# The order of the sums into the first three output tiles of W2, in the 8-tile segments of an MLP

## The chip, the cores and the metric

The kernel runs on one NeuronCore of a Trainium2 chip. The metric is the time of one execution on the device, in microseconds (us), as the median of several runs. A second view is one execution taken by the hardware profiler; all rows below are from that one.

## What is computed

One inference step of a four-layer backbone over 384 tokens (256 latent, 128 context) of width 1024. Layer 0 and 3 mix tokens with a bidirectional state-space layer (S5), layer 1 with neighbourhood attention, layer 2 with grouped-query attention. After each mixer stands the same MLP, and the change lies in it:

```python
def sqrelu_mlp(h, w1, w2):
    a = jax.nn.relu(h @ w1)
    return (a * a) @ w2
...
xp = xp + p_g2 * sqrelu_mlp(hp, mlp_w1[i], mlp_w2[i])
xs = xs + s_g2 * sqrelu_mlp(hs, mlp_w1[i], mlp_w2[i])
```

`w1` is 1024 x 4096, `w2` is 4096 x 1024, all in float32. `h` is the RMS-normed residual stream with scale and shift, `g2` a gate; both come from the conditioning vector (adaLN).

## The kernel before

Features lie on the 128 partitions, the 384 tokens along the free dimension, so the 1024 features of the residual stream `x` are 8 tiles of 128 x 384 and the 4096 hidden features 32 tiles. Each float32 operand is held as two exact parts, a rounded one (`hi`) and the rest (`lo`), and each product is three matmuls (`mm3`, L225: hi x hi, hi x lo, lo x hi, at L227, L228, L229).

Weights come in chunks of 128 x 1024 (`chunk`, L215): SyncE loads one into a `raw` buffer, ScalarE (ACT) casts it to `whi` (L221), VectorE (DVE) subtracts to get `wlo` (L93, the helper of all tensor-tensor operations). There are five raw buffers, which the adaLN weights (`ada`, L163) share, four of `whi` and four of `wlo`.

`mlp` (L385) goes over the hidden features in segments. In layers 0 and 3 there are two segments of 16 hidden tiles. In layers 1 and 2 there are four segments of 8, since tables of the second S5 layer are made beside them (`s5_spill`, L879, on DVE, GpSimd, ACT and PE) and take the space. A segment has two halves:

- W1: for each of its hidden tiles, one chunk of W1 times `h` (24 matmuls into one PSUM bank), then `normed` (L328): DVE multiplies by 1/rms (`nt`) and copies the shift (`nb`), ACT takes the ReLU. DVE squares it (`asq`), and `split` (L231) makes `ahi` (ACT, L235) and `alo` (DVE). These are the squared tiles, a[0] to a[7] in a segment of 8.
- W2: for each of the 8 output tiles f, one chunk of W2 per 8 squared tiles: 24 matmuls, a[0] to a[7] in order, into one bank. Then `residual` (L360; the instructions `x<-mm,mod,x` of L111) adds gate times the bank to `x`. In the last segment of a layer `final` (L280) follows for each tile: ACT and DVE make the next layer's scaled input and the sum of squares (`sq`, `acc`). Where the next layer is S5 (after layer 2), ACT makes `hs` (L294), and after tiles 3 and 7 PE sorts four of them into chunks (`pick`, L357).

From layer 0's mixer on, three PSUM banks serve these sums in turn (`mm`, L239). A bank is free again when DVE has read it: by `nb` in W1, by `residual` in W2. The order of instructions on each engine is set when the program is built, by a scheduler that follows the order of the code closely; every engine runs its own list in order, and an instruction that waits holds up the rest of its list.

Of the kernel before, what the change touches and what calls it, by code (L numbers as in the profile page):

```python
# [18 lines left out]
PSUM = bass.MemoryType.PSUM  # L19
DRAM = bass.MemoryType.DRAM  # L20

P = 128
D = 1024
KT = D // P
# [8 lines left out]
# S5: chunks of Q steps, NC chunk columns (latent 0-15, context 0-15, latent 16-31)  # L33
# [5 lines left out]
# groups per scan; output tiles of the GLU whose first half of the rows comes early  # L39
# [4 lines left out]
# batches of E and of C of the second S5 layer that are made beside the MLP of a layer  # L44
SPILL = {0: (0, 4), 1: (4, 2), 2: (4, 2)}
# steps of adaLN per step of S5, per projection of the neighbourhood and of the grouped-query attention
FS, FN, FG = 4, 2, 1
# steps of attention per projection
SN, SQ = 4, (3, 5, 3)


class Builder:
# [21 lines left out]
    def psum(self, mm, aux, tab=0, sc=0):  # L74
        """PSUM in banks: sums of projections, all else, tables and scores."""
        if self.ps:
            self.ps.close()
        self.ps = ExitStack()
        self.ps_mm = self.pool(self.ps, f"ps_mm{tab}", mm, space=PSUM)
        self.ps_aux = self.pool(self.ps, f"ps_aux{tab}", aux, space=PSUM)  # L80
        if tab:
            self.ps_tab = self.pool(self.ps, "ps_tab", tab, space=PSUM)
        if sc:
            self.ps_sc = self.pool(self.ps, "ps_sc", sc, space=PSUM)
# [29 lines left out]
    def setup(self):  # L114
# [29 lines left out]
        # the q gains carry the scales of the scores  # L144
# [4 lines left out]
    def streams(self, ap):  # L149
        """The two streams of [P, NTOK]: context columns, latent columns."""  # L150
        return (ap[:, 256:], ap[:, 0:256])

# [21 lines left out]
    def flush(self):  # L174
        """The end of the last group of ada()."""
# [55 lines left out]
    def split(self, pool, src, tag, bufs=None):  # L231
        """src as exact hi + lo."""
        hi = pool.tile([P, NTOK], F32R, name=tag + "hi", tag=tag + "hi", **({"bufs": bufs} if bufs else {}))
        lo = pool.tile([P, NTOK], F32R, name=tag + "lo", tag=tag + "lo", **({"bufs": bufs} if bufs else {}))
        self.nc.scalar.copy(hi[:], src)  # L235
        self.sub(lo[:], src, hi[:].bitcast(F32))
        return hi, lo
# [7 lines left out]
    def proj(self, src, x):  # L245
        """One output tile = chunk^T x over the 8 k-tiles of x."""
        hi, lo = self.chunk(src)
        n = x[0][0].shape[1]
        ps = self.mm_tile()[:, :n]
        for k in range(KT):  # L250
            self.mm3(ps, hi[:, k * P:(k + 1) * P], lo[:, k * P:(k + 1) * P], x[k][0][:], x[k][1][:],
                     k == 0, k == KT - 1)
        return ps

# [17 lines left out]
    def scratch(self, start, n):  # L272
        """n values of the space of the norm's parts, where they aren't in use."""
        return self.sc[:, start:start + n]

    def next_norm(self, l, n):
        """The norm that the residual stream goes to next, built up as its tiles become final."""
        self.nx = {"l": l, "n": n, "acc": None, "parts": None, "h": [], "s5": n == 0 and l % 3 == 0}

    def final(self, k):  # L280
        """x[k] is final: x gain as exact parts, the shifts in two more columns, or as chunks for S5; and the sum of
        squares."""
# [37 lines left out]
    def rstd(self):  # L320
        """1 / rms of every token, on all partitions."""
# [6 lines left out]
    def normed(self, pool, ps, r, func, dst):  # L328
        """dst = func(r * ps + shift) from a projection of the parts that final() makes."""
# [9 lines left out]
    def rsqrt(self, m, r):  # L339
        """(m + EPS)^-1/2: a first value from the tables, one Newton step."""  # L340
# [12 lines left out]
    def pick(self, out, gg, src):  # L353
        """out[(step, channel)] = src(step)[channel of group gg], steps in reverse."""
# [5 lines left out]
    def residual(self, ps, gate, f):  # L360
        """x[f] += gate * ps."""
# [3 lines left out]
    def out_proj(self, src, half, x, l, steps, fill):  # L365
        """x += gate * (W^T o) over half of the heads."""
# [18 lines left out]
    def mlp(self, l):  # L385
        nc = self.nc
        with ExitStack() as ctx:
# [17 lines left out]
            for half in range(npart):  # L405
                a = []
                for f in range(seg):
# [6 lines left out]
                    step()  # L414
                for f in range(KT):
                    ps = self.mm_tile()[:, :NTOK]
                    for q in range(seg // KT):
                        hi, lo = self.chunk(self.i["w2"][l, half * seg // KT + q, f])
                        for k in range(KT):
                            kk = q * KT + k  # L420
                            self.mm3(ps, hi[:, k * P:(k + 1) * P], lo[:, k * P:(k + 1) * P], a[kk][0][:], a[kk][1][:],
                                     kk == 0, kk == seg - 1)
                    self.residual(ps, gate, f)
# [7 lines left out]
    def head_rstd(self, pool, raws, kind):  # L431
        """1 / rms over the head dim of up to four raw [P, NTOK] tiles."""
# [9 lines left out]
    def head_norm(self, raw, r, j, gain, kind, t):  # L442
        """t = raw r gain, r that of the j-th tile."""
# [7 lines left out]
    def pipeline(self, items):  # L451
        """Pairs of functions, of which the first runs one ahead: steps that other work is interleaved with."""
# [7 lines left out]
    def steps(self, n):  # L460
        """n steps of the attention that runs beside the projections, and the fill of adaLN."""
# [11 lines left out]
    def value_flip(self, raws, v, first):  # L473
        """v[tok, t, feature] from features by tokens."""
# [3 lines left out]
    def softmax_tail(self, p, total):  # L478
        """p *= 1 / total."""
# [3 lines left out]
    def flip(self, p, n, dst):  # L483
        """dst[key, n, q] = transposes of p [q, n * P]."""
# [117 lines left out]
    def gqa(self, l):  # L602
        nc, i = self.nc, self.i
        with ExitStack() as ctx:
# [13 lines left out]
            def project(first, n, st):  # L618
                """The tiles of k (2) and q (8): projected, then normed, turned and used in steps."""
# [90 lines left out]
    def exp(self, pool, out, x):  # L710
        """exp(x) by 2^n e^r, x within float32's range of exponents."""
# [40 lines left out]
    def s5_tables(self, tp, wide, slot, pe, pc, a8):  # L752
        """Discretised parameters: powers of the step in the order of each direction, for E with B's factor; the matrix of
        Q steps. wide: space for 34 G values."""
# [21 lines left out]
        # f = (A - 1) / lambda  # L776
# [14 lines left out]
        # the order of the steps: the first 64 partitions run forward  # L791
# [16 lines left out]
    def make_e(self, pool, slot, b, pe, work, kf, kp, dd, et):  # L808
        """E[(step, channel), g, r, (direction, state)] = A^j B of GB groups, steps in reverse; and into DRAM the
        products Re(C A^j B) within a chunk, one row of 16 values per (distance, channel)."""  # L810
# [24 lines left out]
        # two groups per product, of which the diagonal blocks count  # L835
# [28 lines left out]
    def make_c(self, cr, b, pc, ca, t):  # L864
        """ca = (Re, -Im) of C A^j."""
# [13 lines left out]
    def s5_spill(self, slot, first, ebs, cbs):  # L879
        """The tables of a later S5 layer, kept in DRAM: steps that other work is interleaved with. The parameters come  # L880
        first, then E and C of some groups."""
# [55 lines left out]
    def s5(self, l, slot):  # L937
# [5 lines left out]
        # places in the scratch space: what final() makes, then the reversed chunks of the second half and y; sel;  # L943
        # the reversed chunks of the first half, then the states that y is made from; kp and d, or sums of states
# [114 lines left out]
    def s5_u(self, pool, u, make=None):  # L1059
        """u[(step, channel), g, chunk], steps in reverse: from x's chunks in layer 0, from those of x gain else."""  # L1060
# [45 lines left out]
    def s5_states(self, ssb, b, et, u, ur, s):  # L1106
        """S[c] = sum over the steps of a chunk of A^j B u for GB groups (columns 48-63 of a group belong to the next)."""
# [28 lines left out]
    def s5_scan(self, pool, s, a8):  # L1136
        """h[c] = A^Q h[c - 1] + S[c] in place: the first value of each stream, then its chunks (latent from 0, context
        from 33); the backward half holds them in reverse."""
# [13 lines left out]
    def s5_out(self, pool, b, ca, tz, u, s, hy, gsb, k):  # L1152
        """The outputs of GB groups: from the state before each chunk and from the chunk itself."""
# [41 lines left out]
    def glu_sums(self, slot, f, halves, k):  # L1195
        """Both output tiles of f over halves of the rows."""
# [12 lines left out]
    def glu_first(self, slot, f, k, part):  # L1209
        """The first half of the rows' share in f's output tiles, and the bias."""  # L1210
# [46 lines left out]
def chunks(w):  # L1257
    """[K * 128, N * 128] weights as [N, 128, K * 128]: one output tile per chunk."""
# [4 lines left out]
def half_chunks(w):  # L1263
    """[1024, N * 256] weights as [N, 2, 128, 4 * 256]: two output tiles over half of the rows per chunk."""
# [4 lines left out]
def lay_out(inp):  # L1269
# [13 lines left out]
    # neighbourhood attention  # L1283
# [18 lines left out]
    # grouped-query attention  # L1302
# [27 lines left out]
    # S5: partitions are (direction, state) or, for the chunks, (step, channel)  # L1330
# [47 lines left out]
```

## Time and profile before

| | us |
|---|---|
| median of 3 runs | 2106.98 |
| lowest and highest run | 2102.32, 2116.06 |
| span of the profiled execution, first to last instruction | 2104.6 |

For the profiled execution the page gives the span; what lies around it is not shown, and the span is 2.4 us under the median. PE is its matmul unit, PEld the loading of weights into it. A row of a timeline has the start, the duration, engine, line, operation, tiles out<-in, and in brackets the idle time before it and what ended it. A PE matmul of 384 columns has a duration of some 0.34 us, but the next one starts after about half of that, so time is counted from start to start. W2 of the eight 8-tile segments begins at 895.3, 974.8, 1054.3 and 1127.2 us (layer 1) and at 1362.6, 1441.4, 1520.9 and 1593.6 us (layer 2).

### The profile page before, as it was taken

Reading aid. Unit: us, or ns where it says so; the run is one execution under the profiler, and the core shown is the slowest. Engines: PE = TensorE matmul, PEld = TensorE weight load, DVE = VectorE, ACT = ScalarE, POOL = GpSimd, SP = SyncE. Lnnn points to the kernel's source line nnn. Section 1 sums busy time; section 2 is a strip of 40 time slices with the busy share of each in tenths; the row PEclk is TensorE's granted clock in tenths of the full one; section 3 lists DMA queues with packets and bytes.
Section 4 is the critical chain, followed back from the end, with each engine's and each line's share of the span. In section 5 each row is a group of like instructions: output and inputs, shape, how many; then the busy total and the mean of one; then the engine's idle time right before and its main releaser. Section 6 shows DMA issues by size and latency. Waiting matters only on the chain. (4 is left out here: it accounts for less than half of the span.)

```text
span 2104.6 us, 35187 instructions
## 1 busy us (share of the span) xinstructions
PE 1980.7 (94%) x13490; PEld 1747.3 (83%) x13490; DVE 1368.2 (65%) x3070; ACT 1029.4 (49%) x2112; POOL 216.4 (10%) x180
## 2 busy tenths in 40 slices
PE   5886899999999999999999999999999878999999
PEld 2554799999987777998999877998997657999999
DVE  7899669856445556856658566856665396674562
ACT  4664656335355555634435555534434477553441
POOL 4443210400000000001111000002111000000000
PEclk8997999999999999999999999999999999999999
DMA  7756654443365555634334532533444575333331
GB/s 286 234 199 238 233 182 152 152 170 120 128 233 192 177 179 193 230 121 154 125 132 163 172 114 98 179 131 128 142 149 156 165 281 221 121 126 125 124 131 67
DMA packets 130823, 348.45 MB, mean 166 GB/s; under 512 B 12800, under 2 KB 48544, under 8 KB 128608
## 3 DMA queue, kind: packets, MB, share of 16 engines
q1 hardware_dynamic: 124160, 338.55, 46.8%
q0 software_dynamic: 1712, 4.05, 0.6%
q10 hardware_dynamic: 4784, 3.61, 0.5%
q8 instruction: 107, 1.75, 0.3%
q14 instruction: 60, 0.49, 0.1%
HBM read 323.22 MB, written 22.94 MB: 164 GB/s over the span
## 5 line engine op out<-in xcount | busy, mean ns | idle before, releaser
L221 ACT CAST whi<-raw 128x1024 fp32r<-128x1024 f32 x340 | 356.4, 1049 | 486.4 <-PE mm L228 422.6
L93 DVE TENSOR_TENSOR wlo<-raw,whi 128x1024 fp32r<-128x1024 f32 x340 | 445.2, 1310 | 197.2 <-ACT whi L221 196.3
L227 PE MATMUL mm<-h,whi 128*128 128x386 f32 x1312 | 453.4, 346 | 0.0
L229 PE MATMUL mm<-h,wlo 128*128 128x386 f32 x1312 | 448.2, 342 | 0.0
L228 PE MATMUL mm<-h,whi 128*128 128x386 f32 x1312 | 446.9, 341 | 0.0
L227 PE MATMUL mm<-ahi,whi 128*128 128x384 f32 x1024 | 350.2, 342 | 10.3 <-ACT ahi L235 10.3
L229 PE MATMUL mm<-ahi,wlo 128*128 128x384 f32 x1024 | 349.3, 341 | 2.8 <-DVE wlo L93 2.8
L228 PE MATMUL mm<-alo,whi 128*128 128x384 f32 x1024 | 349.8, 342 | 1.7 <-DVE alo L93 1.6
L227 PEld LDWEIGHTS mm<-h,whi 128*128 128x128 f32 x1312 | 246.7, 188 | 21.7 <-issue 16.7
L228 PEld LDWEIGHTS mm<-h,whi 128*128 128x128 f32 x1312 | 248.3, 189 | 5.0 <-issue 3.7
L229 PEld LDWEIGHTS mm<-h,wlo 128*128 128x128 f32 x1312 | 247.4, 189 | 5.3 <-issue 4.0
L111 DVE SCALAR_TENSOR_TENSOR x<-mm,mod,x 128x128 f32<-128x128 f32 (+1 forms) x256 | 95.4, 412 | 204.8 <-PE mm L229 204.3
L227 PEld LDWEIGHTS mm<-ahi,whi 128*128 128x128 f32 x1024 | 195.3, 191 | 13.3 <-ACT ahi L235 12.6
L229 PEld LDWEIGHTS mm<-ahi,wlo 128*128 128x128 f32 x1024 | 195.3, 191 | 5.0 <-DVE wlo L93 3.4
L228 PEld LDWEIGHTS mm<-alo,whi 128*128 128x128 f32 x1024 | 195.2, 191 | 5.1 <-DVE alo L93 5.1
L163 PE MATMUL ada<-raw,silu 128*2 128x256 f32 x1536 | 127.1, 407 | 21.1 <-DMA raw<-in_ada_w 16.5
L93 DVE TENSOR_TENSOR nt<-mm,rstd 128x384 f32<-128x384 f32 x164 | 90.6, 553 | 68.1 <-PE mm L229 67.5
L337 ACT ACTIVATE relu<-nt,nb 128x128 f32<-128x128 f32 (+1 forms) x256 | 102.1, 447 | 46.3 <-DVE nb L335 45.9
L235 ACT CAST ahi<-asq 128x384 fp32r<-128x384 f32 x128 | 65.4, 513 | 119.2 <-DVE asq L93 118.8
L93 DVE TENSOR_TENSOR alo<-asq,ahi 128x384 fp32r<-128x384 f32 x128 | 73.0, 572 | 50.3 <-ACT ahi L235 50.2
L163 PEld LDWEIGHTS ada<-raw,silu 128*2 128x2 f32 x1536 | 31.4, 85 | 77.4 <-issue 32.2
L227 PE MATMUL mm<-k,whi 128*128 128x384 f32 x256 | 89.1, 352 | 6.0 <-DVE k L93 2.1
(376 smaller groups left out, 3019.1 us busy)
## 6 DMA issues: line engine op xcount, KB each, us to landing
raw<-in_w SPq DMA_DIRECT2D x256, 512.0 KB, 3.5
raw<-in_ada_w SPq DMA_DIRECT2D x192, 512.0 KB, 4.7
raw<-in_glu SPq DMA_DIRECT2D x32, 512.0 KB, 5.5
tz<-kdr SPq DMA_DIRECT2D x16, 512.0 KB, 5.8
dca<-ca SPq DMA_DIRECT2D x8, 1024.0 KB, 4.3
raw<-in_na_wqk SPq DMA_DIRECT2D x16, 512.0 KB, 4.1
det<-et SPq DMA_DIRECT2D x32, 256.0 KB, 2.6
et<-det SPq DMA_DIRECT2D x32, 256.0 KB, 5.7
```

The costliest lines, as they stand in the source:

```text
L93: self.nc.vector.tensor_tensor(out, a, b, op=op)
L111: self.nc.vector.scalar_tensor_tensor(out, a, s, b, op0=op0, op1=op1)
L163: nc.tensor.matmul(ps[32 * j:32 * j + 2], self.silu[:, k, :], raw[:, 256 * j:256 * j + 256], start=(k == 0), stop=(k == KT - 1))
L221: nc.scalar.copy(hi[:], raw[:])
L227: mm(out, whi, xhi, start=first, stop=False)
L228: mm(out, whi, xlo, start=False, stop=False)
L229: mm(out, wlo, xhi, start=False, stop=last)
L235: self.nc.scalar.copy(hi[:], src)
L337: nc.scalar.activation(o, z, func, bias=b[:, s:s + 1])
```

## The change

In a segment of 8 squared tiles (layers 1 and 2, eight segments in all), the first three output tiles of W2 are opened together: each is summed over a[0] to a[5], one tile after the other, and only then over a[6] and a[7], again one after the other. Tiles 3 to 7, and the segments of 16 in layers 0 and 3, keep their order. The three open tiles hold three banks and three pairs of `whi` and `wlo` until their last two squared tiles are in. The number of matmuls, chunks and other instructions is the same.

```diff
+OPEN, LATE = 3, 2
...
+                opened = OPEN if seg == KT else 0
+                sums = {}
+                for f in range(opened):
+                    sums[f] = self.down(half, f, seg, a, l, range(0, seg - LATE))
                 for f in range(KT):
-                    ps = self.mm_tile()[:, :NTOK]
-                    for q in range(seg // KT):
-                        hi, lo = self.chunk(self.i["w2"][l, half * seg // KT + q, f])
-                        for k in range(KT):
-                            kk = q * KT + k
-                            self.mm3(ps, hi[:, k * P:(k + 1) * P], lo[:, k * P:(k + 1) * P], a[kk][0][:], a[kk][1][:],
-                                     kk == 0, kk == seg - 1)
-                    self.residual(ps, gate, f)
+                    ps = self.down(half, f, seg, a, l, range(seg - LATE, seg), *sums[f]) if f in sums else \
+                        self.down(half, f, seg, a, l, range(seg))
+                    self.residual(ps[0], gate, f)
                     step()
                     if half == npart - 1:
                         self.final(f)
...
+    def down(self, half, f, seg, a, l, tiles, ps=None, w=None):
+        ps = self.mm_tile()[:, :NTOK] if ps is None else ps
+        w = {} if w is None else w
+        for kk in tiles:
+            q, k = divmod(kk, KT)
+            if q not in w:
+                w[q] = self.chunk(self.i["w2"][l, half * seg // KT + q, f])
+            hi, lo = w[q]
+            self.mm3(ps, hi[:, k * P:(k + 1) * P], lo[:, k * P:(k + 1) * P], a[kk][0][:], a[kk][1][:], kk == 0, kk == seg - 1)
+        return ps, w
```

In the order of the changed program the line numbers are two higher for the same code (L229 to L231 are the three matmuls, L95 and L113 stand for L93 and L111). On PE, in the first 8-tile segment of layer 1, the first output tile before the change goes through all eight squared tiles; ahi_9348 is a[5], ahi_9391 a[6], the names after the arrow are operands, the one before it is the bank's tile:

```order
L227 MATMUL mm_9438<-ahi_9348,whi_9441 128x384
L228 MATMUL mm_9438<-alo_9349,whi_9441 128x384
L229 MATMUL mm_9438<-ahi_9348,wlo_9442 128x384
L227 MATMUL mm_9438<-ahi_9391,whi_9441 128x384
L228 MATMUL mm_9438<-alo_9392,whi_9441 128x384
L229 MATMUL mm_9438<-ahi_9391,wlo_9442 128x384
L227 MATMUL mm_9438<-ahi_9434,whi_9441 128x384
```

After the change, at the end of the second open tile's first part (mm_9463), a[0] (ahi_9133) of the third open tile (mm_9488) follows a[5]:

```order
L229 MATMUL mm_9463<-ahi_9348,whi_9466 128x384
L230 MATMUL mm_9463<-alo_9349,whi_9466 128x384
L231 MATMUL mm_9463<-ahi_9348,wlo_9467 128x384
L229 MATMUL mm_9488<-ahi_9133,whi_9491 128x384
L230 MATMUL mm_9488<-alo_9134,whi_9491 128x384
L231 MATMUL mm_9488<-ahi_9133,wlo_9492 128x384
```

The first use of a[6] has moved from place 19 of the 192 matmuls of W2 to place 55, that of a[7] from 22 to 58.

On DVE, in the same W2, the additions to `x` and the making of `wlo` take turns before the change:

```order
L93 TENSOR_TENSOR alo<-asq,ahi 128x384
L111 SCALAR_TENSOR_TENSOR x<-mm,mod_5_6554,x 128x128
L111 SCALAR_TENSOR_TENSOR x<-mm,mod_5_6554,x 128x256
L93 TENSOR_TENSOR wlo<-raw,whi 128x1024
L111 SCALAR_TENSOR_TENSOR x<-mm,mod_5_6554,x 128x128
L111 SCALAR_TENSOR_TENSOR x<-mm,mod_5_6554,x 128x256
L93 TENSOR_TENSOR wlo<-raw,whi 128x1024
```

After it, tile 0's addition still comes first, then the fifth chunk's `wlo`, then two additions and two `wlo`:

```order
L95 TENSOR_TENSOR alo<-asq,ahi 128x384
L113 SCALAR_TENSOR_TENSOR x<-mm,mod_5_6554,x 128x128
L113 SCALAR_TENSOR_TENSOR x<-mm,mod_5_6554,x 128x256
L95 TENSOR_TENSOR wlo<-raw,whi 128x1024
L113 SCALAR_TENSOR_TENSOR x<-mm,mod_5_6554,x 128x128
L113 SCALAR_TENSOR_TENSOR x<-mm,mod_5_6554,x 128x256
L113 SCALAR_TENSOR_TENSOR x<-mm,mod_5_6554,x 128x128
L113 SCALAR_TENSOR_TENSOR x<-mm,mod_5_6554,x 128x256
L95 TENSOR_TENSOR wlo<-raw,whi 128x1024 x2
```

One `wlo` has moved behind the addition of tile 2.

On DVE in the last segment of layer 2, where `final` follows (`acc` is the sum of squares), before the change:

```order
L111 SCALAR_TENSOR_TENSOR x<-mm,mod_5_8869,x 128x128
L111 SCALAR_TENSOR_TENSOR x<-mm,mod_5_8869,x 128x256
L93 TENSOR_TENSOR wlo<-raw,whi 128x1024
L263 TENSOR_TENSOR acc<-sq 128x384
L111 SCALAR_TENSOR_TENSOR x<-mm,mod_5_8869,x 128x128
L111 SCALAR_TENSOR_TENSOR x<-mm,mod_5_8869,x 128x256
L93 TENSOR_TENSOR wlo<-raw,whi 128x1024
L263 TENSOR_TENSOR acc<-acc,sq 128x384
L111 SCALAR_TENSOR_TENSOR x<-mm,mod_5_8869,x 128x128
```

(the first addition shown is tile 1's), and after it (from tile 2's):

```order
L113 SCALAR_TENSOR_TENSOR x<-mm,mod_5_8869,x 128x128
L113 SCALAR_TENSOR_TENSOR x<-mm,mod_5_8869,x 128x256
L95 TENSOR_TENSOR wlo<-raw,whi 128x1024
L265 TENSOR_TENSOR acc<-sq 128x384
L95 TENSOR_TENSOR wlo<-raw,whi 128x1024
L265 TENSOR_TENSOR acc<-acc,sq 128x384
L113 SCALAR_TENSOR_TENSOR x<-mm,mod_5_8869,x 128x128
L113 SCALAR_TENSOR_TENSOR x<-mm,mod_5_8869,x 128x256
```

Two `wlo` and two `acc` now stand between the additions of tiles 2 and 3. The orders of GpSimd and of SyncE's loads are as before.

## Rows read from the trace of the kernel before

**Rows 1.** Page, part 2: granted PE clock in 40 slices, in tenths of full.

```profile
PEclk8997999999999999999999999999999999999999
```

**Rows 2.** Waits of PE from 893 to 1640 us: total us, times, longest us.

```profile
PE mm L227 <- ACT ahi L235: 10.3, 6, 2.2
```

**Rows 3.** Windows, 16 us from each W2 start: us, PE busy (matmuls), clock, DMA share, GB/s.

```profile
895.30:911.30 16.00, 11.97 (x58) 0.89 0.39 132
974.80:990.80 16.00, 16.00 (x92) 1.00 0.34 130
1054.30:1070.30 16.00, 16.00 (x91) 1.00 0.36 129
1127.20:1143.20 16.00, 13.63 (x65) 0.89 0.38 130
1362.60:1378.60 16.00, 12.95 (x61) 0.89 0.37 132
1441.40:1457.40 16.00, 16.00 (x92) 1.00 0.38 130
1520.90:1536.90 16.00, 16.00 (x92) 1.00 0.37 129
1593.60:1609.60 16.00, 13.78 (x59) 0.79 0.46 145
```

**Rows 4.** Timeline of PE, W2 of layer 1's first segment, around a[6] and a[7].

```profile
899.94 0.44 PE L227 MATMUL mm<-ahi,whi 128*128 128x384 f32 x1 [1.34 <-ACT ahi L235]
901.00 0.45 PE L228 MATMUL mm<-alo,whi 128*128 128x384 f32 x1 [0.62 <-DVE alo L93]
...
903.67 1.01 PE L227 MATMUL mm<-ahi,whi 128*128 128x384 f32 x2 [2.06 <-ACT ahi L235]
...
905.76 0.52 PE L227 MATMUL mm<-ahi,whi 128*128 128x384 f32 x1
906.08 0.52 PE L228 MATMUL mm<-alo,whi 128*128 128x384 f32 x1
```

**Rows 5.** Timeline of PE, W2 of layer 1's second segment: end of tile 0.

```profile
978.46 0.34 PE L227 MATMUL mm<-ahi,whi 128*128 128x384 f32 x1
978.79 0.45 PE L228 MATMUL mm<-alo,whi 128*128 128x384 f32 x1
979.07 0.33 PE L229 MATMUL mm<-ahi,wlo 128*128 128x384 f32 x1
979.24 0.34 PE L227 MATMUL mm<-ahi,whi 128*128 128x384 f32 x1
```

**Rows 6.** Timeline of DVE, first segment of layer 1, before and in W2.

```profile
892.17 3.43 DVE L93 TENSOR_TENSOR wlo<-raw,whi 128x1024 fp32r<-128x1024 f32 x1
...
901.33 0.14 DVE L335 COPY nb<-mm 128x2 f32<-128x2 f32 x1
901.40 1.21 DVE L93 TENSOR_TENSOR wlo<-raw,whi 128x1024 fp32r<-128x1024 f32 x1
...
903.65 0.56 DVE L93 TENSOR_TENSOR alo<-asq,ahi 128x384 fp32r<-128x384 f32 x1 [0.58 <-ACT ahi L235]
905.68 0.74 DVE L111 SCALAR_TENSOR_TENSOR x<-mm,mod,x 128x128 f32<-128x128 f32 x2 [1.47 <-PE mm L229]
```

**Rows 7.** Timeline of all engines, last segment of layer 2, after W2's tile 3.

```profile
1616.31 1.05 ACT L221 CAST whi<-raw 128x1024 fp32r<-128x1024 f32 x1 [1.98 <-PE mm L228]
...
1616.38 1.48 PE L163 MATMUL ada<-raw,silu 128*2 128x256 f32 x24
...
1617.26 0.80 ACT L294 ACTIVATE hs<-x,gain 128x128 f32<-128x128 f32 x2
...
1617.97 0.51 ACT L259 ACTIVATE sq<-x 128x384 f32<-128x384 f32 x1
...
1618.76 0.53 PE L357 MATMUL mm<-hs 128*32 128x192 f32 x3
```

**Rows 8.** Page, part 6: loads of the adaLN weights, KB each, us to landing.

```profile
raw<-in_ada_w SPq DMA_DIRECT2D x192, 512.0 KB, 4.7
```

## The prediction

> **What bounds the kernel now.** I read the slices of the page first, then the waits of PE, windows of equal length over the eight W2 starts, and last the timelines of PE, DVE and ACT around them. The granted clock stands at nine tenths or more in nearly every slice [rows 1], so TensorE's rate is not the question at large; what can be won lies in single stops. Of PE's waits in the stretch with the 8-tile segments, the longest group is the one that the change is about: a matmul of W2 that waits for `ahi`, 10.3 us in 6 pieces, up to 2.2 us each [rows 2].
>
> That sum is less than the stops cost. The windows show it [rows 3]: in the 16 us after W2 begins, an undisturbed segment runs 92 matmuls (once 91), one each 16.0 / 92 = 0.174 us. The first and last segment of each layer run 58, 65, 61 and 59, at a mean granted clock of 0.79 to 0.89 instead of 1.00. The other four hardly wait. So half of the eight segments hold nearly all that can be had.
>
> What happens in a disturbed one is in the timeline of layer 1's first segment [rows 4]. After the 18 matmuls on a[0] to a[5], PE waits 1.34 us for the `ahi` of a[6], 0.62 us for its `alo`, and 2.06 us for the `ahi` of a[7]: 4.0 us. Then the clock is at the lower level of 1.2 GHz for a while, after an engine that had stood for 2.06 us: the starts at 905.76 and 906.08 are 0.32 us apart instead of 0.174. In that window 34 matmuls are missing, 34 x 0.174 = 5.9 us; 4.0 were idle, so some 1.9 us belong to the lower clock. The squared tiles are late because DVE is behind: one `wlo` took 3.43 us where another took 1.21 [rows 6], and a[7] is only split at 903.65 + 0.56 = 904.2 us. An undisturbed segment has a small version of the same: between 978.46 and 979.07, at a[7], two steps take 0.33 and 0.28 us, that is 0.27 us too much [rows 5].
>
> **The change, part by part.** Nothing is removed or added on any engine; the matmuls are permuted, and a few instructions of DVE and ACT change places.
>
> *The late use of a[6] and a[7].* Their first uses move back by 36 matmuls, 36 x 0.174 = 6.3 us, with work on a[0] to a[5] of tiles 1 and 2 as cover. In the segment of rows 4, a[6] would now be wanted at 895.3 + 54 x 0.174 = 904.7 and a[7] half a microsecond later, against 904.2 when a[7] is there. That is the one with the longest stop, so the others have more to spare. What goes: the missing matmuls of the four disturbed windows, (92 - 58) + (92 - 65) + (92 - 61) + (92 - 59) = 34 + 27 + 31 + 33 = 125, times 0.174 = 21.8 us [rows 3]. The idle time and the matmuls at the lower clock are both in it, since the windows are long enough to reach back to full pace. And the small step of rows 5, which the undisturbed windows hold as well: 8 x 0.27 = 2.2 us. Together 24.0 us.
>
> *What is late next, in PSUM.* The second and third open tiles take the banks of the last two tiles of W1. The tightest is the third in the segment of rows 6: its bank is read out at 901.33 + 0.14 = 901.5 us, and it is wanted at 895.3 + 36 x 0.174 = 901.6. I allow 0.5 us for the eight segments; the bound is nothing on one side, and on the other 6 us, if each of the four disturbed ones lost 1.5 us there. Tile 3 needs the bank of tile 0. Between tile 0's last matmul and tile 3's first there were 48 matmuls (8.4 us), now 12 (2.1 us). The addition to `x` takes 0.74 us [rows 6] and stands on DVE directly behind the `alo` of a[7], which is done by then; with 0.34 us for the last matmul to end it is through after 1.1 us. So it costs nothing while DVE is free, and up to 2.4 us a segment if a 3.43 us cast got in front.
>
> *Chunks held longer.* The fifth chunk's `whi` reuses the buffer of tile 0's, free after 60 matmuls and no longer after 24; it is wanted at matmul 97. That leaves 36 x 0.174 = 6.3 us for a cast of 1.05 us [rows 7] and a `wlo` of 1.21 us behind the addition of 0.74 us. The sixth and seventh chunks have 10 us and more. Hidden; if ACT and DVE were 3 us behind there, it would show as that wait. The loads behind them are ordered as before and have the same cover.
>
> *The last segment of layer 2.* Here the cover is thin. After tile 3, PE stops summing, runs some adaLN matmuls (1.48 us) and then the picks, which need all of `hs` 0 to 3. Tiles 0 to 2 used to end 4 us apart; now they end 1 us apart, and their casts and scalings queue up. Tile 3 now ends at about 1593.6 + 96 x 0.174 = 1610.3. On ACT, from tile 0's end at 1604.3, stand three casts of 1.05, three `hs` of 0.80 and three `sq` of 0.51 us [rows 7]: 7.1 us, to 1611.4, the third cast ending half a microsecond earlier. From there DVE makes the seventh `wlo` and an `acc` (which has the size of `alo`), adds tile 3 (1.2 + 0.6 + 0.7) [rows 6], and ACT scales it (0.8): about 1614. Picks began at 1618.76, 2.4 us after the adaLN matmuls that follow tile 3 (1616.38); now it would be 1614 - 1610.3 = 3.7 us. The third adaLN load waits for the sixth `wlo`: three additions and two `wlo` after 1604.3, 2.2 + 2.4 us, are 1608.9, and with 4.7 us to landing [rows 8] it comes at about the same 1614. So 1.3 us is given back here; between nothing and, if PE's stand brings the lower clock with it as in the segment of rows 4, 1.3 + 1.9 = 3.2 us.
>
> In the last segment of layer 1 the same queue forms on DVE, but the next stage needs it only after tile 7, and by then it has drained: each tile brings 3.3 us of DVE work (an addition and a scaling like it of 0.74 each, a `wlo` of 1.2, an `acc` of 0.56) in the 4.2 us of its 24 matmuls.
>
> *Sum.* 24.0 - 0.5 - 1.3 = 22.2 us less. All of it is on the path, since PE goes on from each W2 to the next W1 and on to the next mixer without other slack. The profiled span of 2104.6 us becomes 2082.4; the median of the runs lies 2.4 us above the span, and the same added gives 2084.8, or 2085 us. That is 1.05% under 2107, and 1% (21 us) is about what a measurement of this kernel can tell from no change, so the forecast stands right at that line.
>
> **The rivals.**
>
> *The wait moves on.* PE no longer waits for DVE at a[7], but DVE is as far behind as before; PE overtakes it and waits at the next thing that it makes, the `wlo` of chunks 4 to 6 or a bank. For it: in the disturbed segments DVE works on a backlog right up to 904.2 [rows 6]. Against it: the margins above, 1 to 6 us, hold in each place that I followed. It would give back half of the gain: 2107 - 11 = 2096 us.
>
> *The bank of tile 0.* The addition to `x` gets behind a slow `wlo` of 3.43 us [rows 6]. Then tile 3 waits 1.1 + 3.43 - 2.1 = 2.4 us in every segment, and the lower clock follows, 1.9 us as above. 8 x 4.3 = 34 us against 22 won: 2119 us, slower. It decides from 22 / 8 = 2.8 us in each segment, 0.9 of them waiting. Against it: on DVE's list nothing but the `alo` of a[7] stands before that addition.
>
> *Short bursts on changing banks.* Going from bank to bank after 18 and 6 matmuls leaves PE small gaps, and the clock falls to the lower level over the whole stretch of 72 matmuls: 72 x (0.32 - 0.174) = 10.5 us in each of eight segments, 84 - 22 = 62 us slower, 2169 us. Against it: the change of tile after 24 matmuls costs nothing now, 979.07 to 979.24 is a step like any other [rows 5]. The Trainium skill describes such a case in "TensorE: Matmul & The Clock Gate", section "A second HAM failure mode: psum-queue depth-cycling": a kernel that cycled through PSUM banks had small idle times between groups of matmuls, and its clock kept falling and rising. By that rule this rival would hold; rows 5 do not bear it out for a plain change of bank, and no row shows groups as short as 6.
>
> **How the numbers follow.** The forecast has 0.72, its own range 2079 to 2091 us: from 24 us plus a little for runs that scatter, to 6 us lost at the banks and 3 us at the picks with the scatter. The wait that moves on has 0.17, the two slower rivals 0.03 and 0.02, and 0.06 is left for a larger gain. The range of eight in ten takes in most of the first rival: 2077 to 2099. Faster by over 1% means under 2086: a little over half of the forecast (0.40) and the larger gain, 0.46. Slower by over 1% is the last rival and a bad form of the second, 0.03. Within 1%: 0.51.
>
> **What would show it.** Right: the eight windows of rows 3 all run 90 to 93 matmuls at clock 1.00, and the waits of PE for `ahi` vanish from the list. The first step is wrong if PE still stands at a[6] or a[7]; the second if the matmul that opens tile 3 waits for DVE's `x`; the third if tiles 4 to 6 wait for `whi` or `wlo`; the fourth if the picks of the last segment begin less than 2.4 or more than 5 us after tile 3. The whole is wrong if PE's waits go, but the span does not follow, because a later stage takes the time back.

## The result, and the profile after

The changed kernel took 2081.97 us as the median of 4 runs (2079.26 to 2084.41), the kernel before 2107.07 beside it (4 runs, 2102.32 to 2116.06): a ratio of 0.9882, 95% interval 0.9861 to 0.9902. That is 25 us less; 22.2 were forecast, 2085 us. The profiled execution took 2083.82 us at a span of 2082.0, 22.6 us under the span of before.

The same windows as in [rows 3], 16 us from the start of each W2 of 8 tiles, in the changed kernel:

```profile
895.70:911.70 16.00, 16.00 (x93) 1.00 0.39 133
969.00:985.00 16.00, 16.00 (x93) 1.00 0.28 98
1048.10:1064.10 16.00, 16.00 (x93) 1.00 0.27 96
1120.50:1136.50 16.00, 16.00 (x94) 1.00 0.38 129
1352.70:1368.70 16.00, 16.00 (x93) 1.00 0.35 123
1426.00:1442.00 16.00, 16.00 (x94) 1.00 0.29 97
1505.40:1521.40 16.00, 16.00 (x93) 1.00 0.25 94
1577.70:1593.70 16.00, 16.00 (x93) 1.00 0.44 145
```

All eight run at the pace of an undisturbed one, and the granted clock is 1.00 in each. Together they hold 93 + 93 + 93 + 94 + 93 + 94 + 93 + 93 = 746 matmuls where [rows 3] hold 610: 136 x 0.174 = 23.7 us. The slices of the clock read as in [rows 1]; single stops don't show there. In the waits of PE from 885 to 1630 us the group of [rows 2] is gone; the longest are these:

```profile
PE aux L868 <- POOL kf L864: 9.3, 8, 1.5
PE aux L718 <- DVE rs_a L113: 1.9, 1, 1.9
PE ada L165 <- DMA raw<-in_ada_w: 1.8, 1, 1.8
```

DVE itself is no earlier than before. In layer 1's first segment it reads out the bank that the third open tile takes, and splits a[7], at these times:

```profile
901.36 0.14 DVE L337 COPY nb<-mm 128x2 f32<-128x2 f32 x1
903.67 0.56 DVE L95 TENSOR_TENSOR alo<-asq,ahi 128x384 fp32r<-128x384 f32 x1 [0.58 <-ACT ahi L237]
```

That is 904.2 us for a[7], as in [rows 6], and W2 began at 895.7 in place of 895.3. PE wants a[7] at 895.7 + 57 x 0.174 = 905.6 now, and the bank, free at 901.5, at 895.7 + 36 x 0.174 = 902.0. Neither makes it wait.

The bank of tile 0, the subject of the second rival, shows in the timelines of PE and DVE in the same segment. Tile 0's last matmul:

```profile
905.97 0.34 PE L231 MATMUL mm<-ahi,wlo 128*128 128x384 f32 x1
```

and on DVE the addition to `x` and the next `wlo`:

```profile
906.35 0.74 DVE L113 SCALAR_TENSOR_TENSOR x<-mm,mod,x 128x128 f32<-128x128 f32 x2 [2.12 <-PE mm L231]
907.26 1.23 DVE L95 TENSOR_TENSOR wlo<-raw,whi 128x1024 fp32r<-128x1024 f32 x1 [0.17 <-ACT whi L223]
```

The addition is through at 907.09, 1.1 us after the last matmul began, and tile 3 wants the bank at 895.7 + 72 x 0.174 = 908.2. In the last segment of layer 2, where the cover was called thin, PE after tile 3:

```profile
1594.28 0.33 PE L231 MATMUL mm<-ahi,wlo 128*128 128x384 f32 x1
1594.54 1.05 PE L165 MATMUL ada<-raw,silu 128*2 128x256 f32 x16
1597.39 0.61 PE L165 MATMUL ada<-raw,silu 128*2 128x256 f32 x8 [1.80 <-DMA raw<-in_ada_w]
1597.82 0.87 PE L359 MATMUL mm<-hs 128*32 128x192 f32 x8
```

The picks begin 1597.82 - 1594.54 = 3.3 us after the adaLN matmuls, against 2.4 before [rows 7]. What PE waits for is the adaLN load; ACT had its last `hs` done at 1596.07 + 0.90 = 1596.97:

```profile
1596.07 0.90 ACT L296 ACTIVATE hs<-x,gain 128x128 f32<-128x128 f32 x2 [0.54 <-DVE x L113]
```

### The profile page after: what moved, and what is told of

It reads as the page before. It is cut to its first block, busy times and chain, and to the rows that moved or that the text cites. A ratio compares the mean times of both kernels' runs of the same rounds, so it can differ in the third digit from the quotient of the medians.

```text
span 2082.0 us, 35201 instructions
## 1 busy us (share of the span) xinstructions
PE 1965.7 (94%) x13490; PEld 1735.6 (83%) x13490; DVE 1366.8 (66%) x3070; ACT 1029.6 (49%) x2112; POOL 216.6 (10%) x180
## 5 line engine op out<-in xcount | busy, mean ns | idle before, releaser
L95 DVE TENSOR_TENSOR wlo<-raw,whi 128x1024 fp32r<-128x1024 f32 x340 | 444.3, 1309 | 194.8 <-ACT whi L223 194.2
L229 PE MATMUL mm<-h,whi 128*128 128x386 f32 x1312 | 453.3, 346 | 0.0
L231 PE MATMUL mm<-h,wlo 128*128 128x386 f32 x1312 | 448.3, 342 | 0.0
L231 PE MATMUL mm<-ahi,wlo 128*128 128x384 f32 x1024 | 345.1, 337 | 3.2 <-DVE wlo L95 3.2
L229 PE MATMUL mm<-ahi,whi 128*128 128x384 f32 x1024 | 345.0, 337 | 0.0
L230 PE MATMUL mm<-alo,whi 128*128 128x384 f32 x1024 | 344.2, 336 | 0.6 <-DVE alo L95 0.6
L229 PEld LDWEIGHTS mm<-h,whi 128*128 128x128 f32 x1312 | 246.7, 188 | 21.7 <-issue 16.2
L231 PEld LDWEIGHTS mm<-h,wlo 128*128 128x128 f32 x1312 | 247.4, 189 | 5.4 <-issue 4.0
L113 DVE SCALAR_TENSOR_TENSOR x<-mm,mod,x 128x128 f32<-128x128 f32 (+1 forms) x256 | 94.6, 411 | 187.2 <-PE mm L231 186.7
L231 PEld LDWEIGHTS mm<-ahi,wlo 128*128 128x128 f32 x1024 | 192.0, 188 | 5.5 <-DVE wlo L95 3.8
L229 PEld LDWEIGHTS mm<-ahi,whi 128*128 128x128 f32 x1024 | 192.1, 188 | 0.8 <-issue 0.7
L95 DVE TENSOR_TENSOR nt<-mm,rstd 128x384 f32<-128x384 f32 x164 | 90.6, 553 | 68.1 <-PE mm L231 67.8
L95 DVE TENSOR_TENSOR alo<-asq,ahi 128x384 fp32r<-128x384 f32 x128 | 73.0, 572 | 50.4 <-ACT ahi L237 50.2
L229 PE MATMUL mm<-k,whi 128*128 128x384 f32 x256 | 89.9, 355 | 5.9 <-DVE k L95 2.1
```

What stands on the lines that cost most here:

```text
L95: self.nc.vector.tensor_tensor(out, a, b, op=op)
L113: self.nc.vector.scalar_tensor_tensor(out, a, s, b, op0=op0, op1=op1)
L229: mm(out, whi, xhi, start=first, stop=False)
L230: mm(out, whi, xlo, start=False, stop=False)
L231: mm(out, wlo, xhi, start=False, stop=last)
```

## The experiments

Twelve kernels, in three sets; in each set the kernel before ran on the same chip, and each ratio is to it. The theory: the gain is the later use of a[6] and a[7] in the four segments where DVE is late (the disturbed ones: the first and last of layers 1 and 2), the lower clock after those stops included. The rivals: the new order helps in every segment; short bursts on changing banks cost time; only the count of open tiles matters.

**Only the disturbed segments, and only the others.**

```diff
-                opened = OPEN if seg == KT else 0
+                opened = OPEN if seg == KT and half in (0, npart - 1) else 0
```

The second kernel has `0 < half < npart - 1` there.

> Only the first and the last segment of layers 1 and 2 are opened, the four in between keep the order of before. Theory (the gain is the later use of a[6] and a[7] where DVE is behind, with the lower clock after those stops): the four opened windows run 93 matmuls, the other four 91 or 92, and all but 4 x 0.25 = 1 us of the gain stays: about 2083 us, ratio to before 0.988 to 0.990. Rival (the later use helps every segment alike, or the new order of DVE and of the loads does it): half of the gain, about 2094 us, ratio 0.994.

> The counterpart: only the four segments in between are opened. Theory: the disturbed windows stay at 58 to 65 matmuls and a mean granted clock of 0.79 to 0.89; only the small steps at a[7] go, about 1 us: 2106 us, ratio 0.999 to 1.000. Rival (all segments alike): about 2094 us, ratio 0.994.

Measured: 2085.89 us, ratio 0.9891 (0.9870 to 0.9913), for the first; 2109.16 us, ratio 0.9995 (0.9979 to 1.0012), for the second. The first has windows of 92, 93, 93, 93 where it is opened and 91 or 92 elsewhere. Two of the disturbed windows of the second, which has them in the order of before:

```profile
893.60:909.60 16.00, 12.29 (x53) 0.79 0.42 132
...
1593.60:1609.60 16.00, 13.76 (x67) 0.89 0.45 146
```

The gain sits in the four disturbed segments; opening the others alone can't be told from no change.

**Two open tiles.**

```diff
-OPEN, LATE = 3, 2
+OPEN, LATE = 2, 2
```

> Two output tiles are opened instead of three, so a[6] is wanted 36 and a[7] 39 matmuls after W2 begins instead of 54 and 57. Theory: in the changed kernel a[7] was cast 7.97 us after W2 began in layer 1's first segment and 6.2 to 6.4 us in the three other disturbed ones; wanted at 39 x 0.174 = 6.8 us, it stops PE by 1.2 us, and its lower part by 0.4 more, in that one segment alone; 1.6 us more than the changed kernel, 3.5 if the lower clock follows, and up to 1 us less at the picks of layer 2, since tiles 0 and 1 end earlier: 2082 to 2086 us, ratio 0.988 to 0.990. Rival (the gain grows with the number of open tiles, whatever is late): two thirds of it at most half, 2090 us or more.

Measured: 2086.77 us, ratio 0.9897 (0.9872 to 0.9921), span 2081.4. PE in the first segment, where a[7] is wanted three matmuls after a[6]:

```profile
902.03 0.34 PE L231 MATMUL mm<-ahi,wlo 128*128 128x384 f32 x1
903.36 0.44 PE L229 MATMUL mm<-ahi,whi 128*128 128x384 f32 x1 [0.99 <-ACT ahi L237]
903.95 0.44 PE L230 MATMUL mm<-alo,whi 128*128 128x384 f32 x1 [0.15 <-DVE alo L95]
904.23 0.34 PE L231 MATMUL mm<-ahi,wlo 128*128 128x384 f32 x1
```

From start to start 1.33 and 0.59 us instead of 0.174 each: 1.6 us lost, as worked out, and full pace right after it. By the starts of their matmuls the other three disturbed segments lose 0.15 to 0.5 us. The median lies 0.8 us above the range given, the ratio inside it, and its interval overlaps that of the changed kernel (0.9861 to 0.9902). Two tiles are nearly enough; the third is a reserve for the one segment that is latest.

**Only a[7] late.**

```diff
-OPEN, LATE = 3, 2
+OPEN, LATE = 3, 1
```

> Three tiles are opened, but over a[0] to a[6], with only a[7] left for the end. Theory: a[7] is covered by 63 matmuls, a[6] by 18 as before. In the changed kernel a[6] was cast 4.2 us after W2 began in layer 1's first segment, its lower part done at 5.3; wanted at 3.1 and 3.3 us, they stop PE by 2.0 us; in the three other disturbed segments the cast is in time (2.95 to 3.16) and the lower part 0.4 us late: 3.2 us. Tile 3 opens 6 matmuls after tile 0 ends instead of 12, so the bank of tile 0 is wanted just when its addition ends: 0 to 0.2 us in each of eight segments. Together 3 to 5 us more than the changed kernel, up to 7 if the lower clock follows: 2085 to 2089 us, ratio 0.989 to 0.992. Rival (a[7] alone was the matter): the time of the changed kernel, 2082. Rival (the bank of tile 0 costs 2 us and more in each segment as soon as it is close): 2100 or more.

Measured: 2096.17 us, ratio 0.9937 (0.9913 to 0.9961); the time is 7 us above the upper end of what was expected. PE in the first segment:

```profile
900.61 0.45 PE L229 MATMUL mm<-ahi,whi 128*128 128x384 f32 x1 [1.35 <-ACT ahi L237]
901.67 0.55 PE L230 MATMUL mm<-alo,whi 128*128 128x384 f32 x1 [0.62 <-DVE alo L95]
902.01 0.52 PE L231 MATMUL mm<-ahi,wlo 128*128 128x384 f32 x1
902.34 0.52 PE L229 MATMUL mm<-ahi,whi 128*128 128x384 f32 x1
902.65 0.52 PE L230 MATMUL mm<-alo,whi 128*128 128x384 f32 x1
```

The 2.0 us of idle time came, the lower clock after it too (steps of 0.31 to 0.34 us), and at the bank of tile 0 each of the eight segments lost 0.12 us. By the starts of the W2s the MLPs lose 8.0 us against the changed kernel, where 3 to 7 were expected. Another 4.6 us are lost behind the picks of layer 2, in the S5 stage: there the program's order puts some adaLN matmuls elsewhere, and PE waits for one of their sums to be read, a wait that the changed kernel doesn't have:

```profile
PE ada L165 <- ACT mrow L172: 4.4, 1, 4.4
```

No run separates that part. What it teaches: a small edit in the MLP changed the scheduler's order in the stage behind it, and an estimate that stops at the edit misses that.

**The three tiles in turn.** The first 54 matmuls go over a[0] of tiles 0, 1, 2, then a[1] and so on:

```diff
-                for f in range(opened):
-                    sums[f] = self.down(half, f, seg, a, l, range(0, seg - LATE))
+                for kk in range(seg - LATE if opened else 0):
+                    for f in range(opened):
+                        sums[f] = self.down(half, f, seg, a, l, (kk,), *sums.get(f, ()))
```

> The first 54 matmuls go over the three open tiles in turn, three matmuls each (a[0] of tile 0, 1, 2, then a[1] ...); a[6] and a[7] stay last, tile by tile. The third bank is then wanted 6 x 0.174 = 1.0 us after W2 begins instead of 6.3. Theory (the later use pays only as long as nothing else is wanted before it is free): in the changed kernel that bank was read out 5.8 us after W2 began in layer 1's first segment and 4.1 to 4.3 us in the three other disturbed ones, 0.9 in the segments between; so PE stops at the opening of tile 2 by 4.8, 3.2, 3.0 and 3.2 us, 14 us together, and up to 4 x 1.9 us more with the lower clock: 2096 to 2104 us, ratio 0.994 to 0.998. Rival (any order that uses a[6] and a[7] last is as good): 2082 us.

Measured: 2107.19 us, ratio 0.9982 (0.9960 to 1.0004): the gain is gone, and the time is 3 us above the upper end of what was expected. The waits of PE now have this on top:

```profile
PE mm L229 <- DVE nb L337: 14.4, 8, 2.5
```

and in its timeline the opening of tiles 1 and 2:

```profile
899.02 0.42 PE L229 MATMUL mm<-ahi,whi 128*128 128x384 f32 x1 [2.25 <-DVE nb L337]
899.27 0.34 PE L230 MATMUL mm<-alo,whi 128*128 128x384 f32 x1
...
902.76 0.66 PE L229 MATMUL mm<-ahi,whi 128*128 128x384 f32 x1 [2.45 <-DVE nb L337]
903.22 0.52 PE L230 MATMUL mm<-alo,whi 128*128 128x384 f32 x1
903.54 0.52 PE L231 MATMUL mm<-ahi,wlo 128*128 128x384 f32 x1
```

14.4 us of stops at banks that W1's last tiles still hold, where 14 were worked out, and the lower clock behind them. The clock cost more than was allowed for it: the four disturbed windows hold 48, 63, 55 and 66 matmuls, 140 fewer than four times 93, which is 24.4 us. Less the 14.4 of waiting that leaves 10.0 us, 2.5 a segment, where at most 1.9 was expected. a[6] and a[7] are used as late as in the changed kernel; the lateness of DVE is met at the banks instead. So tile by tile is not a matter of taste: it is what has the third bank wanted after 36 matmuls and not after 6.

**Single matmuls on alternating banks.** The last 12 matmuls of tiles 1 and 2:

```diff
+                    if f == 1 and opened:
+                        self.alternate([sums[1], sums[2]], a, seg)
...
+        for kk in range(seg - LATE, seg):
+            for n in range(3):
+                for ps, w in tiles:
+                    self.nc.tensor.matmul(ps, w[0][n == 2][:, cols], a[kk][n == 1][:],
```

> The last 12 matmuls of tiles 1 and 2, on a[6] and a[7], alternate between the two banks, one matmul each, in every segment; all else as in the changed kernel. Theory: a change of bank costs nothing, the eight windows keep 93 matmuls at clock 1.00, 2080 to 2085 us, ratio 0.987 to 0.989. Rival (short bursts on changing banks leave gaps): with steps of 0.27 us instead of 0.174 in each of the 96 places 9 us more, 2091; with the lower clock after it 1.9 us a segment more, 2106.

Measured: 2086.83 us, ratio 0.9887 (0.9871 to 0.9903); the time is 2 us above the range given for the theory, the ratio inside it. The alternating pairs in PE's timeline and the first two windows:

```profile
908.54 0.51 PE L443 MATMUL mm<-ahi,whi 128*128 128x384 f32 x2
908.89 0.51 PE L443 MATMUL mm<-alo,whi 128*128 128x384 f32 x2
909.24 0.51 PE L443 MATMUL mm<-ahi,wlo 128*128 128x384 f32 x2
```

```profile
898.00:914.00 16.00, 16.00 (x93) 1.00 0.40 131
971.20:987.20 16.00, 16.00 (x93) 1.00 0.31 97
```

A pair every 0.35 us is a matmul every 0.174: a change of bank after each single one costs nothing, and the clock stays at 1.00. The Trainium skill's "TensorE: Matmul & The Clock Gate", section "A second HAM failure mode: psum-queue depth-cycling", tells of a kernel whose clock fell in small pauses between groups on changing banks; by that rule these windows would hold fewer matmuls. Here the change of bank alone does not make such pauses.

**Why DVE is late.** The trace of before holds the answer in rows that the prediction had not put side by side. GpSimd, in W1 of layer 1's last segment, makes the tables of the second S5 layer:

```profile
1113.63 2.60 POOL L874 TENSOR_TENSOR ca<-ca,ct 128x1024 f32<-128x1024 f32 x1 [9.83 <-DVE ca L93]
1119.00 2.67 POOL L877 TENSOR_TENSOR ca<-ca,ct 128x1024 f32<-128x1024 f32 x1 [2.77 <-DVE ca L93]
```

and DVE at the same time:

```profile
1114.42 2.89 DVE L93 TENSOR_TENSOR wlo<-raw,whi 128x1024 fp32r<-128x1024 f32 x1
...
1119.85 2.90 DVE L93 TENSOR_TENSOR wlo<-raw,whi 128x1024 fp32r<-128x1024 f32 x1
```

GpSimd ends at 1116.23 and 1121.67, the two `wlo` at 1117.31 and 1122.75: each 1.08 us later, nearly the whole of an undisturbed `wlo` (1.21). Beside the 3.43 us `wlo` of [rows 6] GpSimd is at work too:

```profile
891.86 2.66 POOL L826 TENSOR_TENSOR ei<-ei,et 128x1024 f32<-128x1024 f32 x1 [4.91 <-DVE et L93]
```

GpSimd ends at 894.52, that `wlo` at 895.60, again 1.08 us later. So `wlo` was not slowed down, it stood until GpSimd was through. The Trainium skill states the same in "SBUF — State Buffer", section "Who interferes with whom": the two engines share one pair of ports under an exclusive lock. These rows agree. Both kernels of this test keep the order of sums of the kernel before; `beside` holds in the MLPs of layers 1 and 2. The first leaves GpSimd's additions and subtractions out, so its tables are incomplete:

```diff
-        nc.gpsimd.tensor_tensor(er, er, t1, op=ALU.subtract)
+        if not self.beside:
+            nc.gpsimd.tensor_tensor(er, er, t1, op=ALU.subtract)
```

(and three more like it); the second keeps them, on DVE:

```diff
+        (nc.vector if self.beside else nc.gpsimd).tensor_tensor(er, er, t1, op=ALU.subtract)
```

> The kernel before, but in the MLPs of layers 1 and 2 the tables of the second S5 layer are made without GpSimd's additions and subtractions of 128 x 1024 (E and C then hold one product instead of two). Theory (DVE is late because each of its wlo beside such a GpSimd instruction takes 2.9 to 3.4 us instead of 1.21, about 1.7 more, two of them ahead of a disturbed W2): in the last segments of both layers a[7] comes 3.4 us earlier and the stops of 2.6 to 2.8 us go; windows 65 and 59 become 90 or more. In layer 1's first segment 3.9 us earlier, 58 becomes about 85. In layer 2's first segment four more table products of 1.21 us fit into DVE's list ahead of a[7], so little changes there. Some 85 matmuls or 15 us: about 2092 us, ratio 0.993. Rival (DVE is late by its own table products, whatever GpSimd does): windows as before, ratio 0.999 to 1.000.

> The kernel before, with the additions and subtractions of the tables on DVE (1.21 us each) instead of GpSimd, in the MLPs of layers 1 and 2; the output is complete. Theory: ahead of a disturbed W2 DVE loses twice 1.7 us in a wlo beside GpSimd; twice 1.21 us of its own instead makes a[7] about 1 us earlier. The stops of 2.6 to 4.0 us become about 1 us shorter: windows of 65 to 75, 4 to 8 us of gain, 2099 to 2104 us, ratio 0.996 to 0.998. Rival (it is the single long wlo that decides, the sum of DVE's work hardly): windows over 85 and a gain of 15 us or more, ratio 0.993 or less. Rival (only the sum of DVE's work counts, which grows by 10 us over both layers): no gain, ratio 1.000 or more.

Measured without them: 2091.36 us, ratio 0.9903 (0.9881 to 0.9926). Its windows of the first and last segments:

```profile
899.70:915.70 16.00, 15.68 (x90) 1.00 0.41 133
...
1125.50:1141.50 16.00, 16.00 (x92) 1.00 0.37 120
1359.80:1375.80 16.00, 15.11 (x86) 1.00 0.43 133
...
1586.80:1602.80 16.00, 16.00 (x92) 1.00 0.45 137
```

58, 65, 61, 59 became 90, 92, 86, 92, and the mean `wlo` of the two layers fell from 1.359 to 1.222 us:

```profile
L95 DVE TENSOR_TENSOR wlo<-raw,whi 128x1024 fp32r<-128x1024 f32 x141 | 172.4, 1222 | 38.4 <-ACT whi L223 38.3
```

The cause of the lateness is shown. DVE's list ahead of a[7] holds nothing less: in the last segments two products of the tables change places, in the first ones one and three products come to it, and a[7] is still ready 1.9 to 3.8 us earlier. The expectation that layer 2's first segment would hardly change was wrong.

Measured with them on DVE: 2088.06 us, ratio 0.9913 (0.9891 to 0.9934), windows of 89, 92, 89, 92 in the disturbed segments. The medians differ by 18.7 us; my 4 to 8 were far too few, and that is the first rival's number. I had counted the two GpSimd instructions closest to W2. But in the last segment of layer 1 four fall into W1, and the first two hold DVE for 1.7 and 2.2 us: 7.3 us in all, against 4 x 1.22 = 4.9 on DVE itself. The order of DVE's list changed with it as well. The a[7] of that segment came 3.1 us earlier (3.9 instead of 7.0 us after W2's start), not 1. How much of that is the sum and how much the new order is not separated.

**Both cures, and what is left.** The changed kernel with the tables' additions on DVE in layers 1 and 2 (from the set of the tiles in turn; the other three kernels stem from one later set); then in layer 0 too; then with the two small additions of `kf` on DVE as well; then, on top, two open tiles in the last segment of layer 2:

```diff
+                opened = 0 if seg != KT else 2 if l == 2 and half == npart - 1 else OPEN
```

> The changed kernel with those additions and subtractions on DVE (1.21 us each) instead of GpSimd (2.4 to 2.9 us each, beside which a wlo loses 1.7). Theory: PE doesn't wait for DVE in the 8-tile segments any more, so what DVE saves is not on the path: 2080 to 2085 us, ratio 0.987 to 0.990, windows 93. If the longer run of DVE work collides with a[7] again, windows fall below 90 and the time goes to 2085 to 2092. Rival (DVE still sets the time somewhere in the MLPs): 3 us or more faster than the changed kernel, under 2079.

> The changed kernel with the tables' additions and subtractions on DVE in the MLPs of layers 0, 1 and 2. In layer 0 PE waits 3.2 us for wlo and 0.6 for alo in the first W2, which takes 71.4 us against 67.4 in the second. Theory (the same GpSimd instructions make DVE late there): the 4 us go, about 2078 us, ratio 0.985 to 0.987. Rival (DVE is late there by its own work): as the run with layers 1 and 2 alone, ratio 0.987 to 0.988, or slower by up to 3 us.

> As the run before it, and the two small additions of kf (128 x 32) on DVE too. PE waits for GpSimd's kf eight times, 9.3 us together; the two take 0.90 and 0.41 us on GpSimd. Theory (DVE does each in 0.2 us, and PE waits only for what stands ahead of them on DVE's list, a wlo of 1.21 at most): between 8 us less and no change, most likely 4 us less than the run before it, ratio 0.983 to 0.986. Rival (DVE's list holds them up for longer than GpSimd takes): 0 to 5 us more.

> As the run before it, but with two open tiles instead of three in the last segment of layer 2. Theory (the casts and scalings of three tiles that end 1 us apart hold up the adaLN load and the picks): the picks begin about 2.4 us after tile 3 instead of 3.3, and the wait for the adaLN load of 1.8 us shrinks to about 0.6, as in the run with two open tiles everywhere; 1 us less than the run before it, which the times alone can't tell. Rival (the queue on ACT and DVE is as long): picks 3 us or more after tile 3.

| | us | ratio to before |
|---|---|---|
| tables on DVE, layers 1 and 2 | 2083.84 | 0.9872 (0.9854 to 0.9889) |
| layer 0 too | 2081.59 | 0.9893 (0.9869 to 0.9917) |
| `kf` too | 2071.08 | 0.9844 (0.9821 to 0.9866) |
| two open tiles in the last segment too | 2067.44 | 0.9811 (0.9788 to 0.9834) |

The first is as fast as the changed kernel, as the theory has it: later use and punctual making are two cures for one stop and don't add up. The second removes layer 0's wait in the trace (its first W2 takes 67.1 instead of 71.4 us), but its time shows no gain. Its profiled execution lost 7.7 us beside the changed kernel's on the way from layer 0's second W2 to layer 1's first, part of it at the lower clock; it is one of two runs of six at 2090 us, and the other four took 2079 to 2082. So the trace speaks for the theory, but the times do not show its 2078 and fit the rival's missing gain as well. The third takes away the eight waits for `kf`, which were the longest left: 10.5 us less than the second by the medians, more than the 9.4 that the waits held and than the 0 to 8 expected. The fourth begins its picks 2.0 us after the adaLN matmuls start, the third 3.4, and the adaLN load keeps PE waiting 0.4 us instead of 1.9. The waits of PE that its trace lists from 860 to 1600 us, the MLPs of layers 1 and 2 and the stage between them:

```profile
PE aux L722 <- DVE rs_a L115: 1.9, 1, 1.9
PE aux L464 <- DVE hrstd L97: 1.1, 1, 1.1
PE ada L167 <- DMA raw<-in_ada_w: 0.4, 1, 0.4
```

From the first W2 of layer 1 to the last of layer 2 it takes 669.8 us, the changed kernel 682.0. The intervals of the last two overlap, so the last step is shown by its trace, not by its time. By the ratios to before the last kernel is faster than both kernels of the study.

## Why the prediction was right, point by point

*The late use.* Right in place and size: 24.0 us forecast, 23.7 by the windows. The runs with only the outer and only the inner segments show that nearly all of it comes from the four disturbed ones, as [rows 3] said; a[7] was ready at 904.2 and wanted no sooner, as worked out from [rows 4]. One price beside the sum was too low. The 1.9 us for the lower clock is the first segment's alone; by the same working the four windows of [rows 3] stand idle for 64 - 52.3 = 11.7 of their 21.8 us, so the lower clock took 10.1, 2.5 a segment. The sum counts missing matmuls and does not need that price, but the rivals and the expectation for the tiles in turn used it. That the cover of 6.3 us is needed only once, 3.1 being nearly enough elsewhere, is shown by two open tiles.

*The banks.* 0.5 us were allowed and none was lost. That they were the next thing to be late is shown by the tiles in turn: the same banks, wanted 15 and 30 matmuls sooner (2.6 and 5.2 us), cost 14.4 us of waiting.

*Chunks held longer.* No wait for `whi` or `wlo` in tiles 4 to 6; hidden, as said.

*The last segment of layer 2.* 1.3 us forecast, 0.9 measured. The forecast had `hs` and the adaLN load arrive together; the load was last, by 0.4 us.

*The sum.* By the profiled executions: the starts of the first and last W2 lie 698.3 us apart before and 682.0 after, 16.3 less over seven segments; 6.7 less from there to the next W1, 5.0 of it up to the picks; 0.4 lost ahead of the first. That is 22.6, beside 22.2 forecast. Inside it are 1.6 us lost in the grouped-query attention and 1.7 won in the S5 stage, which the prediction did not have and which the change was not meant to touch. No run shows what the S5 stage won its part by. That the two nearly cancel is luck, and so is part of the closeness of 22.6 to 22.2. The medians differ by 25.1; the runs of before alone spread over 14 us, and the interval of the ratio (21 to 29 us) holds 22.2.

*The rivals.* The wait that moves on did not come about in this order, but it is real: the tiles in turn are that rival. Tile 0's bank had its 1.1 us to spare (the slow instruction feared there, called a cast, is a `wlo`, a subtraction on DVE); with only a[7] late the reserve is used up, and it costs 0.12 us a segment. The bursts on changing banks are refuted by the alternating kernel.

## What to carry to other kernels

When an in-order engine stops at the last of several operands, let it work first on what it has, in as many sums as there are free buffers; count in steps when each next thing is wanted, the buffers of those sums first, since a late producer is met there again. Windows of equal length over all repetitions of a stage show which repetitions can gain at all. And ask why the producer is late: here the cause lay on a third engine and could be removed by itself for most of the same gain.

## What was not expected of the hardware

*The same stop, with and without a lower clock.* In the grouped-query attention PE waits for `rs_a` in every trace, 1.85 to 1.91 us. In the changed kernel:

```profile
1263.01 1.60 PE L718 MATMUL aux<-g_pt,gqa_v 128*128 128x256 f32 x4 [1.90 <-DVE rs_a L113]
```

and in the kernel before:

```profile
1274.62 1.10 PE L703 MATMUL aux<-g_pt,gqa_v 128*128 128x256 f32 x4 [1.85 <-DVE rs_a L111]
```

The same four matmuls take 1.60 and 1.10 us, and the mean granted clock is 0.88 from 1258 to 1272 us in the changed kernel and 1.00 from 1270 to 1284 in the kernel before. In 5 of the 14 traces the clock was at the lower level after this stop, in 9 it was not. With the tiles in turn a stop of 2.25 us was followed by full pace and one of 2.45 us, 3.7 us later, by the lower level. So an estimate of what a stop costs has two values; I took 1.9 us for the lower clock where it came, the disturbed segments paid 2.5 on average, and 1.6 us of the changed kernel's profiled time went to a place that the change doesn't touch.

*A `wlo` beside GpSimd stands until GpSimd is through*, ending 1.08 us after it in the three pairs of rows above.

*Where the runs scatter.* The first stage, from the start to layer 0's first W2, which these edits hardly touch, took 374.8 to 381.6 us in the fourteen traces: 7 us, more than most of the differences discussed here.
